# A hybrid decoder layer: a first phase ordered by a table of due times, attention's products weighted after the sum, w_out kept in the token tiles

## The chip, the cores and the metric

The kernel runs on one core of a Trainium2 chip. Five engines work from queues of their own: PE multiplies matrices (PEld is its loading of weights), DVE and ACT work on vectors, POOL on vectors and some DMAs, SP issues most DMAs. The metric is the device time of one execution in microseconds, the median of three runs.

## The reference

The layer works on 1024 tokens of width 1024, in fp32. It has an attention group and a gating group in parallel, an output projection with a residual, and then a mixture of experts, in which each token goes to 4 of 32 experts. What bears on this change is attention, which has three branches (compressed, selected, window) whose outputs are weighted by gates:

```python
h = rmsnorm(x, norm1_g)
z = h @ w_in                       # 1024 x 2328, split into q, k and v of three branches, gates, u, v
...
p_cmp = masked_softmax(s, dist_c >= 0)
o_cmp = jnp.einsum('bgrqc,bgcd->bgrqd', p_cmp.astype(vc.dtype), vc)
...
o_sel = jnp.einsum('bgrqk,bgqkd->bgrqd', p.astype(v_g.dtype), v_g)
...
o_win = jnp.einsum('bgrqk,bgkd->bgrqd', p.astype(v_w.dtype), v_w)
o = gt[..., 0:1] * o_cmp + gt[..., 1:2] * o_sel + gt[..., 2:3] * o_win
...
mixed = jnp.concatenate([rmsnorm(o_attn, out_norm_attn_g), rmsnorm(o_gm, out_norm_gm_g)], axis=-1)
x = x + mixed @ w_out
x = x + moe(rmsnorm(x, norm2_g), w_router, b_router, w_gate_up, b_gate_up, w_down, b_down)
```

There are 8 query heads of width 64 in two groups of 4, which share keys and values. With 16 selected blocks of 64 and 1024 tokens every block is selected, so the selected branch is causal attention over all keys; the window branch looks at the last 512.

## The kernel before, in words

Numbers are kept as a pair of f16 (a high part and the rest), so a product of fp32 accuracy takes three f16 matmuls; plain fp32 is used for transposes and small things.

*First phase.* The tokens are eight tiles of 128. `x_tile` normalises and transposes them into `xh` and `xl` (high and low parts). `piece_tile` projects them through w_in in nine pieces of columns, 24 matmuls of some 256 columns per tile and piece (lines 405 to 407). Keys and queries are normalised, transposed and stored (`stack_half`, `turn_half`).

*Attention* runs in units: one `Unit` is a group of 4 heads, a query tile i and a branch, 48 in all, in the order of `ORDER`. For each head `score` has two matmuls (lines 857, 858), and DVE adds distances and takes the running extreme (861); ACT takes the exponential with its sum (841). `weigh` divides the gate by the sum (878 to 880), and `scale` multiplies the four heads' probabilities by it, each on the engine that `SCALE` names (894 ACT, 896 DVE or POOL). `back` then does each block of 128 keys, 148 blocks in all: four fp32 transposes (910), an f16 high part on ACT (914) and low part on DVE (918), and the product with values (928, 929), with the values as the weights that PE loads and 512 columns (4 heads x 128 queries) streamed. The three branches of a group and tile add up in one PSUM bank; `finish` takes it out (942), transposes it back to tokens (946) and adds the two halves of the values' pair on DVE (950).

*Rows.* When both groups of a tile are done, `Rows` normalises, projects through w_out (`part`, lines 1255 to 1257), adds the residual, normalises again and routes. `out_row` (1045 to 1049) loads the eight blocks of w_out, scales and splits them into `wo`, a buffer that is opened in the place of the token tiles after the last projection (`open_out`). Gating runs beside it, on the columns u and v of the projection; its result goes to DRAM (`og_d`, line 559).

*Experts.* A second plan, of the same kind, does the experts (lines 1665 to 1817). Its weights come in as fp32 into five buffers, four of which lie in `wo`.

*What sets the order.* `Plan` records every operation with its engine, a cost, a due time, what it reads and writes, and the slots of rings that it uses: `psS` (3 PSUM banks for scores and projections), `psT` (3, for transposes), `psO` (2, for products), `par` (an arena of 15 blocks of probabilities) and others. `run` lays the operations out: among those that can start first on their engine, the one with the least due time. What it yields is each engine's queue, which the chip executes in order. Due times are written out in the code from a few constants (`TP`, `FS`, `AHEAD`, `US`, `WD`).

Of the kernel before, what the change touches and what calls it, by code (L numbers as in the profile page):

```python
# [61 lines left out]
ARENA = 15  # L62
# [8 lines left out]
SCALE = [['act', 'pool', 'pool', 'pool'], ['pool', 'dve', 'pool', 'act'], ['dve', 'dve', 'dve', 'act']]  # L71
MAXB = 64
LAND = 10.0

# [10 lines left out]
class Plan:  # L85
# [3 lines left out]
    def __init__(self, rings):  # L89
        self.rings = {k: (n, dyn, []) for k, (n, dyn) in rings.items()}  # L90
        self.ops, self.last, self.readers, self.scope = [], {}, {}, ()

# [19 lines left out]
    def op(self, eng, cost, fn, due, r=(), w=(), use=(), lag=None):  # L112
        i = len(self.ops)
        deps, take, after = set(), [], []
# [19 lines left out]
        self.ops.append((eng, cost, fn, due, deps, take, slots, after, lag))  # L134
# [7 lines left out]
    def run(self):  # L142
# [6 lines left out]
        end, free, avail = [0.0] * n, {}, {}  # L149
# [6 lines left out]
        def ready(i):  # L156
            eng, _, _, _, deps, take, _, after, _ = ops[i]
# [13 lines left out]
        for _ in range(n):  # L171
# [11 lines left out]
            eng, cost, fn, _, _, take, slots, _, _ = ops[i]  # L183
# [15 lines left out]
def layer_kernel(ctx: ExitStack, tc: tile.TileContext, x, norm1_g, w_in, q_norm_g, k_norm_g, cmp_pos,  # L199
# [22 lines left out]
    def rstd_of(dst, ss, n):  # L222
# [58 lines left out]
                     ph=(4, 1), pl=(4, 1), ob=(2, 1), mx=(8, 1), su=(6, 0), ptc=(4, 0), dup=(2, 0), par=(ARENA, 0),  # L281
                     m=(2, 0), ogt=(1, 0), x1=(2, 0), xn=(1, 0), xt=(1, 0), xp=(1, 0), s2=(2, 0), jo=(1, 1)))
# [10 lines left out]
    def rms(dst, src, n, tok, due, r):  # L293
        op("dve", 0.1, lambda: nc.vector.tensor_scalar(dst(), src(), 1.0 / n, EPS, op0=ALU.mult, op1=ALU.add), due, r=r, w=[tok])
        op("act", 0.1, lambda: nc.scalar.activation(dst(), dst(), AF.Sqrt), due, r=[tok], w=[tok])
# [3 lines left out]
    st = ExitStack()  # L299
    xtp = pool(st, "xtp")  # L300
    xh = xtp.tile([P, KD, T], F16, name="xh")
    xl = xtp.tile([P, KD, T], F16, name="xl")
# [28 lines left out]
    def x_tile(a):  # L331
        due = 1.5 * a
# [12 lines left out]
        op("act", 1.0, stat, due + 3, r=[x_], w=[ss])  # L345
        rms(lambda: rstd1[:, a:a + 1], lambda: ss1[:, a:a + 1], D, ("rstd1", a), due + 3.5, [ss])
        op("dve", 0.62, lambda: nc.vector.tensor_scalar(x_.t, x_.t, rstd1[:, a:a + 1], None, op0=ALU.mult), due + 4,
# [4 lines left out]
    def x_half(a, h, x_, due):  # L352
        b, tk = plan.slot("psT"), ("x", a, h)
        k, c = slice(4 * h, 4 * h + 4), slice(a * P, (a + 1) * P)
# [6 lines left out]
        op("act", 0.5, lambda: nc.scalar.activation(xh[:, k, c], four(b), AF.Copy, scale=SZ), due, r=[b], w=[tk])  # L361
        op("dve", 0.6, lambda: nc.vector.scalar_tensor_tensor(xl[:, k, c], four(b), SZ, xh[:, k, c], op0=ALU.mult,
                                                              op1=ALU.subtract), due, r=[b, tk], w=[tk])

    def piece_half(i, kh):
        _, c0, n, _ = PIECES[i]
# [17 lines left out]
        op("sp", 1.5, load, due - (14 if i else 0), w=[r])  # L384
        op("act", 1.6, hi, due - (8 if i else -3), r=[r, "g1"], w=[ws])
# [5 lines left out]
    def piece_tile(i, a, ws):  # L391
        kind, _, n, o0 = PIECES[i]
# [7 lines left out]
        def run():  # L400
            o = ps_tile(ps, psS)[:, :n]
            for k in range(KD):
                wh, wl = [v[:, k % 4, :n] for v in ws[k // 4].t]
                xa, xb = xh[:, k, a * P:(a + 1) * P], xl[:, k, a * P:(a + 1) * P]
# [7 lines left out]
    def take(kind, o0, a, ps, due):  # L412
        r, rs = 1.0 / (SW * SZ), ("rstd1", a)
        if kind == "v":
            op("act", 0.3, lambda: nc.scalar.activation(PO["vb"][:, a, o0:o0 + 256], ps.t[:, :256], AF.Identity, scale=r), due, r=[ps, rs],
# [3 lines left out]
        elif kind == "kcvc":  # L419
            op("act", 0.3, lambda: nc.scalar.activation(kcvc[:, a].rearrange("p b g d -> p (b g d)"), ps.t[:, :256], AF.Identity,  # L420
# [6 lines left out]
    def take_kv(br, a, ps, due, r, rs):  # L427
# [13 lines left out]
        op("act", 0.6, keys, due, r=[ps, rs], w=[("kv", br, a)])  # L441
# [3 lines left out]
        op("dve", 0.4, sums, due + 1, r=[("kv", br, a)], w=[("ssk", br, a)])  # L445
# [14 lines left out]
    def norms(lo, n, toks, key, due):  # L460
        rms(lambda: rsq[:, :, lo:lo + n], lambda: ssq[:, :, lo:lo + n], DH, ("rsq", key), due, toks)
# [69 lines left out]
    def gating(d0, due, late):  # L531
        def mask():
            nc.vector.tensor_scalar(PO["tril"], jp, 0.0, None, op0=ALU.is_ge)
# [1426 lines left out]
```

## Time and profile before

| | |
|---|---|
| median of 3 runs | 1983.84 us (1983.23 to 1987.50) |
| the profiled execution | 1987.46 us, of which the span is 1985.7 |
| granted clock of PE, mean of the span | 0.98 |
| busy in the span | PE 95%, PEld 85%, DVE 84%, ACT 75%, POOL 41% |
| first phase | to about 640 us; DMA moves 1 to 152 GB/s in its slices |
| experts | the rest; DMA about 300 to 360 GB/s |

Times within the profile are microseconds from the start of the span. "Busy" of PE includes the time in which the last columns of a burst run out, so it is more than the work done. The granted clock is a share of full speed, 2.4 GHz; 0.50 is the level of 1.2 GHz.

### The profile page before, as it was taken

Reading aid. Unit: us, or ns where it says so; the run is one execution under the profiler, and the core shown is the slowest. Engines: PE = TensorE matmul, PEld = TensorE weight load, DVE = VectorE, ACT = ScalarE, POOL = GpSimd, SP = SyncE. Lnnn points to the kernel's source line nnn. Section 1 sums busy time; section 2 is a strip of 40 time slices with the busy share of each in tenths; the row PEclk is TensorE's granted clock in tenths of the full one; section 3 lists DMA queues with packets and bytes.
Section 4 is the critical chain, followed back from the end, with each engine's and each line's share of the span. In section 5 each row is a group of like instructions: output and inputs, shape, how many; then the busy total and the mean of one; then the engine's idle time right before and its main releaser. Section 6 shows DMA issues by size and latency. Waiting matters only on the chain.

```text
span 1985.7 us, 58597 instructions
## 1 busy us (share of the span) xinstructions
PE 1879.5 (95%) x24346; PEld 1680.4 (85%) x24346; DVE 1659.9 (84%) x2876; ACT 1496.9 (75%) x2374; POOL 814.1 (41%) x699
## 2 busy tenths in 40 slices
PE   7999898989897899999999999999999999999996
PEld 6886666655554887899999999999999999999996
DVE  5668778787776899788989999899999999989883
ACT  6558868886653776677778888788888888878884
POOL 0212132354652255344444444344444525446442
PEclk9999999989998899999999999999999999999998
DMA  4320000033123998899999999999999999999993
GB/s 152 91 59 23 12 12 1 22 133 86 65 86 116 297 331 314 290 299 326 331 338 336 338 341 359 338 356 354 358 362 356 352 356 351 346 343 359 358 351 88
DMA packets 244768, 485.77 MB, mean 245 GB/s; under 512 B 20034, under 2 KB 29394, under 8 KB 244498
## 3 DMA queue, kind: packets, MB, share of 16 engines
q1 hardware_dynamic: 230658, 441.19, 63.1%
q0 software_dynamic: 12800, 40.79, 9.1%
q8 instruction: 192, 3.15, 0.6%
q14 instruction: 78, 0.64, 0.1%
q10 hardware_dynamic: 1040, 0.00, 0.0%
HBM read 450.94 MB, written 31.00 MB: 243 GB/s over the span
## 4 chain that ended last, share of the span: by engine, by line
PE 70%; DVE 10%; ACT 8%; DMA 7%; issue 3%; POOL 1%; DVEq 0%; POOLq 0%; SPq 0%; ACTq 0%
PE g L1739 16%; PE g L1740 16%; PE g L1741 16%; DMA wo<-in_w_gate_up_dram 3%; PE s L405 2%; PE s L407 2%; PE s L406 2%; DVE wl L1696 2%; ACT wh L1693 2%; DVE par L861 2%; PE b L910 2%; PE b L1807 2%; DMA wo<-in_w_down_dram 2%; PE b L1665 1%; DMA raw<-in_w_gate_up_dram 1%
## 5 line engine op out<-in xcount | busy, mean ns | idle before, releaser
L1739 PE MATMUL g<-xar,wh 128*128 128x88 f16 (+21 forms) x4096 | 772.3, 229 | 0.6 <-ACT ott L1790 0.6
L1740 PE MATMUL g<-xar,wh 128*128 128x88 f16 (+21 forms) x4096 | 772.5, 229 | 0.0
L1741 PE MATMUL g<-xar,wl 128*128 128x88 f16 (+21 forms) x4096 | 771.9, 229 | 0.0
L1696 DVE SCALAR_TENSOR_TENSOR wl<-wo,wh 128x2048 f16<-128x2048 f32 x308 | 715.2, 2328 | 39.2 <-ACT wh L1693 37.6
L1693 ACT ACTIVATE wh<-wo 128x2048 f16<-128x2048 f32 x308 | 625.9, 2036 | 160.3 <-PE g L1740 85.7
L1740 PEld LDWEIGHTS <-wh 128*128 128x128 f16 x6144 | 601.4, 98 | 15.4 <-issue 4.3
L1739 PEld LDWEIGHTS <-wh 128*128 128x128 f16 x6144 | 601.8, 98 | 10.7
L1741 PEld LDWEIGHTS <-wl 128*128 128x128 f16 x6144 | 601.3, 98 | 10.7
L1767 POOL TENSOR_TENSOR aar<-t,aar 128x136 f16<-128x136 f32 (+21 forms) x256 | 360.3, 1426 | 477.6 <-ACT aar L1765 447.9
L1739 PE MATMUL g<-aar,wh 128*128 128x120 f16 (+21 forms) x2048 | 385.1, 228 | 3.1 <-DVE t L1754 3.1
L1741 PE MATMUL g<-aar,wl 128*128 128x120 f16 (+21 forms) x2048 | 385.1, 228 | 0.0
L1740 PE MATMUL g<-aar,wh 128*128 128x120 f16 (+21 forms) x2048 | 385.1, 228 | 0.0
L1754 DVE TENSOR_SCALAR t<-g,bias 128x120 f32<-128x120 f32 (+20 forms) x512 | 170.6, 363 | 33.4 <-PE g L1741 21.4
L1693 ACT ACTIVATE wh<-raw 128x2048 f16<-128x2048 f32 x76 | 154.7, 2035 | 40.2 <-PE g L1740 23.5
L1696 DVE SCALAR_TENSOR_TENSOR wl<-raw,wh 128x2048 f16<-128x2048 f32 x76 | 176.5, 2322 | 7.8 <-ACT wh L1693 7.4
L1817 POOL DMA_INDIRECT out_dram<-orow,ix x51 | 121.6, 2384 | 146.9 <-ACT orow L1810 82.0
L1635 POOL DMA_INDIRECT xg<-xn_d,ix x51 | 127.0, 2491 | 112.2 <-PE g L1741 35.9
L405 PE MATMUL s<-wh,xh 128*128 128x256 f16 (+1 forms) x576 | 158.8, 276 | 2.8 <-DVE mx L861 1.9
L407 PE MATMUL s<-wh,xl 128*128 128x256 f16 (+1 forms) x576 | 158.6, 275 | 0.1
L406 PE MATMUL s<-wl,xh 128*128 128x256 f16 (+1 forms) x576 | 158.7, 275 | 0.0
L896 POOL TENSOR_SCALAR par<-par,su 128x384 f32<-128x384 f32 (+7 forms) x32 | 60.0, 1884 | 151.9 <-DVE su L880 68.2
L918 DVE TENSOR_TENSOR pl<-b,ph 128x512 f16<-128x512 f32 (+1 forms) x148 | 96.8, 682 | 30.0 <-ACT ph L914 29.5
(388 smaller groups left out, 2888.4 us busy)
## 6 DMA issues: line engine op xcount, KB each, us to landing
wo<-in_w_gate_up_dram SPq DMA_DIRECT2D x205, 1024.0 KB
wo<-in_w_down_dram SPq DMA_DIRECT2D x103, 1024.0 KB
raw<-in_w_gate_up_dram SPq DMA_DIRECT2D x51, 1024.0 KB
raw<-in_w_down_dram SPq DMA_DIRECT2D x25, 1024.0 KB
wr<-in_w_in_dram SPq DMA_DIRECT2D x16, 512.0 KB
xs<-in_x_dram SPq DMA_DIRECT2D x8, 512.0 KB
x<-in_w_out_dram SPq DMA_DIRECT2D x8, 512.0 KB
x<-in_x_dram SPq DMA_DIRECT2D x8, 512.0 KB
```

The lines of the kernel that those rows point to most:

```text
L405: mm(o, xa, wh, start=(k == 0), stop=False)
L406: mm(o, xa, wl, start=False, stop=False)
L407: mm(o, xb, wh, start=False, stop=(k == KD - 1))
L1635: nc.gpsimd.indirect_dma_start(out=xg.t[:w], out_offset=None, in_=xn_d, in_offset=bass.IndirectOffsetOnAxis(ap=ix.t[:w, 0:1], axis=0))
L1693: nc.scalar.activation(ws.v[0], raw_.v, AF.Copy, scale=SW)
L1696: nc.vector.scalar_tensor_tensor(ws.v[1], raw_.v, SW, ws.v[0], op0=ALU.mult, op1=ALU.subtract)
L1739: mm(o, wh, xa, start=(kh == 0 and k == 0), stop=False)
L1740: mm(o, wh, xb, start=False, stop=False)
L1741: mm(o, wl, xa, start=False, stop=(kh == 1 and k == 3))
L1754: nc.vector.tensor_scalar(t.t[:, s, :c], ps[s].t[:, :c], self.bias(2 * h + s), m, op0=ALU.add, op1=o)
L1767: plan.op("pool", 0.9 + c / 440, lambda: nc.gpsimd.tensor_tensor(out=self.a[:, h, 1], in0=t.t[:, 1, :c], in1=self.a[:, h, 0], op=ALU.subtr ...
L1817: self.plan.op("pool", 2.0, lambda: nc.gpsimd.indirect_dma_start(out=out, out_offset=bass.IndirectOffsetOnAxis(ap=ix.t[:w, 0:1], axis=0), ...
```

## The change

Three things change, all in the first phase; the plan of the experts is left alone, except that four of its five fp32 buffers now lie in the token tiles.

1. *Order.* Operations are put in groups (`plan.group()`), and each group has an offset in a table `WHEN`, which is added to its due times (the offsets lie between about -2300 and 1530 us). The costs in the plan are set to other numbers, and a switch of ACT's function table costs 1.29 us in the plan.
2. *Weights.* `scale` is gone. The probabilities are transposed and split unscaled. In the product the probabilities are now what PE loads, and the values (128 columns, both parts of the pair) are streamed: 8 matmuls of 128 columns a block. Each unit has a product bank of its own, in the layout of tokens; `weighted` multiplies it by the ratio on DVE, and `finish` adds three of them and the two halves on POOL. The ring of results has 4 slots, and the arena of probabilities 13 blocks instead of 15.
3. *w_out.* Tokens are kept tile by tile in `xw`, which stays open. `out_row` writes the split w_out over a token tile once the last projection has read it, and loads through the ring of the projection weights.

```diff
-ARENA = 15
+ARENA = 13
-SCALE = [['act', 'pool', 'pool', 'pool'], ['pool', 'dve', 'pool', 'act'], ['dve', 'dve', 'dve', 'act']]
+OB = 4
+WHEN = [
+    1346.1, 299.4, 788.3, -170.5, 1081.8, 114.3, -565.0, 519.3, -380.7, 1232.6, -82.9, 90.6, -610.6, 327.8, 529.5, -374.5, 361.1,
...
+TABLE = 1.29
...
+    def group(self):
+        self.at += 1
...
     def op(...):
         i = len(self.ops)
+        due += self.when[self.at] if self.at < len(self.when) else 0
...
+            if table not in (None, loaded):
+                loaded, cost = table, cost + TABLE
...
-            plan.op("dve", 0.25, ratio, due, r=[("su", su, j) for j in range(4)] + ["gates"], w=[su])
-            for j in range(4):
-                self.scale(j, due)
-
-        def scale(self, j, due):
-            su, nk = self.su, self.nk
-            eng = SCALE[self.br][j]
-            def run():
-                p, w = self.probs(j), su.t[:, j:j + 1]
-                if eng == "act":
-                    nc.scalar.activation(p, p, AF.Copy, scale=w)
-                else:
-                    (nc.gpsimd if eng == "pool" else nc.vector).tensor_scalar(p, p, w, None, op0=ALU.mult)
...
+            plan.op("dve", 0.41 if br else 0.61, ratio, due, r=[("su", su, j) for j in range(4)] + ["gates"], w=[("w", su)], use=[su])
...
             def hi():
-                nc.scalar.activation(ph.t[:n], four(b)[:n], AF.Copy)
+                nc.scalar.activation(ph.t[:n], four(b)[:n], AF.Copy, scale=SP)
             def lo():
-                nc.vector.tensor_tensor(out=pl.t[:n], in0=four(b)[:n], in1=ph.t[:n], op=ALU.subtract)
+                nc.vector.scalar_tensor_tensor(pl.t[:n], four(b)[:n], SP, ph.t[:n], op0=ALU.mult, op1=ALU.subtract)
             def pv():
...
-                mm(o.t, va, ph.t[:n].rearrange("p h t -> p (h t)"), start=st, stop=False)
-                mm(o.t, va, pl.t[:n].rearrange("p h t -> p (h t)"), start=False, stop=en)
+                for j in range(4):
+                    for m, p in enumerate((ph, pl)):
+                        mm(o.t[:, j * P:(j + 1) * P], p.t[:n, j], va, start=st and j + m == 0, stop=en and j + m == 4)
...
-    def finish(g, i, o, due):
+        def weighted(self, due):
+            ob, o, su = self.ob, self.o, self.su
+            def run():
+                ob.t = PO["hp"].tile([P, 4, P], F32, name="ob", bufs=OB)
+                nc.vector.tensor_tensor(out=ob.t, in0=four(o), in1=su.t[:, :, None].to_broadcast([P, 4, P]), op=ALU.mult)
+            plan.op("dve", 0.6, run, due, r=self.parts + [("w", su)], w=[ob], use=[o, su])
+
+    def finish(g, i, units, due):
-        def evac():
-            nc.scalar.activation(ob.t, o.t, AF.Copy, scale=1.0 / (SP * SV))
-        def turn():
-            for j in range(4):
-                nc.tensor.transpose(four(b)[:, j], ob.t[:, j * P:(j + 1) * P], ident)
-        plan.op("dve", 0.65, lambda: nc.vector.tensor_reduce(
...
+        a, b, c = [u.ob for u in units]
+        def last():
+            v = a.t.rearrange("p h (s d) -> p h s d", s=2)
+            nc.gpsimd.tensor_tensor(out=zq[:, i, 256 * g:256 * g + 256].rearrange("p (h d) -> p h d", h=4), in0=v[:, :, 0], in1=v[:, :, 1],
+                                    op=ALU.add)
+        for x in (b, c):
+            plan.op("pool", 1.56, lambda x=x: nc.gpsimd.tensor_tensor(out=a.t, in0=a.t, in1=x.t, op=ALU.add), due, r=[x], w=[a])
+        plan.op("pool", 0.9, last, due, r=[a] + ..., w=[("o", g, i)])
...
+    def wo(k, s):
+        return xw[:, (k + 4) % 8, s].rearrange("p k t -> p (k t)")
     def out_row(k, due):
-        r, g = plan.slot("x1"), gms[:, k:k + 1]
+        r, g, a = plan.slot("wr"), gms[:, k:k + 1], (k + 4) % 8
...
+           w=[("wo", k), ("x", a, 0), ("x", a, 1)])
...
-        PO["wo"] = pool(ctx, "raw").tile([P, 4, 2, 2, D], F16, name="wo")
...
-    raws = [PO["wo"][:, n].rearrange("p s j f -> p (s j f)").bitcast(F32) for n in (2, 3, 0, 1)] + [raw5]
+    raws = [xw[:, 2 * n:2 * n + 2].rearrange("p a s k t -> p (a s k t)").bitcast(F32) for n in range(4)] + [raw5]
```

PE's queue at the first product of the first unit, before (`ph` and `pl` are the parts of the transposed probabilities, `vv` the values, `kcs` and `q` keys and queries, `o` the product's bank):

```order
L910 MATMUL b_2465<-ident_81,par_1604 128x128 x4
L928 LDWEIGHTS vv_103
L928 MATMUL o_2471<-ph_2415,vv_103 128x512
L929 LDWEIGHTS vv_103
L929 MATMUL o_2471<-pl_2456,vv_103 128x512
L857 LDWEIGHTS q3_154
```

The same place now (`xw` is a token tile, `wh` and `wl` projection weights):

```order
L470 LDWEIGHTS xw_119
L470 MATMUL s_2246<-wh_1713,xw_119 128x256
L996 LDWEIGHTS ph_2236
L996 MATMUL o_2278<-vv_103,ph_2236 128x128
L996 LDWEIGHTS pl_2271
L996 MATMUL o_2278<-vv_103,pl_2271 128x128
```

Two products of 512 columns with two loads became eight of 128 with a load each (the last four rows come four times, once for each head).

POOL's queue where attention begins, before (`par` and `ptc` hold probabilities, `su` the ratios; the rows ahead are a normalisation):

```order
L476 TENSOR_TENSOR rsq_106<-nwq_107 128x8x4
L896 TENSOR_SCALAR par_1604<-par_1604,su_1959 128x384 x2
L896 TENSOR_SCALAR ptc_1961<-ptc_1961,su_2004 128x64 x3
L896 TENSOR_SCALAR par_1604<-par_1604,su_2008 128x128 x2
L896 TENSOR_SCALAR ptc_2002<-ptc_2002,su_2014 128x64 x3
L896 TENSOR_SCALAR par_1604<-par_1604,su_2422 128x768 x2
```

The same place now (`ob` are weighted products, `zq` the attention output):

```order
L541 TENSOR_TENSOR rsq_106<-nwq_107 128x8x4
L1025 TENSOR_TENSOR ob_2409<-ob_2409,ob_2528 128x512
L1025 TENSOR_TENSOR ob_2409<-ob_2409,ob_2560 128x512
L1021 TENSOR_TENSOR zq_99<-ob_2409 128x256
L1025 TENSOR_TENSOR ob_2639<-ob_2639,ob_2699 128x512
```

POOL no longer stands between the exponentials and the transposes; it comes after the products.

SP's queue around w_out, before (`wr` projection weights, `og_d` the gated result in DRAM, `ogt` its way back):

```order
L372 DMA wr_3520<-in_w_in_dram 128x4x256
L559 DMA og_d_66<-vb_1618 128x4x512 x2
L1045 DMA x1_5561<-in_w_out_dram 128x1024
L1045 DMA x1_5581<-in_w_out_dram 128x1024
L1143 DMA ogt_5651<-og_d_66 128x512
L1143 DMA ogt_5708<-og_d_66 128x512
L1045 DMA x1_5716<-in_w_out_dram 128x1024
```

The same place now:

```order
L433 DMA wr_3542<-in_w_in_dram 128x4x256
L1123 DMA wr_3586<-in_w_out_dram 128x1024
L1123 DMA wr_3781<-in_w_out_dram 128x1024
L1123 DMA wr_4697<-in_w_out_dram 128x1024
L1123 DMA wr_4815<-in_w_out_dram 128x1024
L1123 DMA wr_4867<-in_w_out_dram 128x1024
L628 DMA og_d_66<-vb_1707 128x4x512
L1123 DMA wr_5026<-in_w_out_dram 128x1024
L1123 DMA wr_5093<-in_w_out_dram 128x1024
L1123 DMA wr_5219<-in_w_out_dram 128x1024
L628 DMA og_d_66<-vb_1707 128x4x512
```

Five loads of w_out stand ahead of the first store of the gated result and three between the two, where before both stores came first.

## Rows read from the trace of the kernel before

**Rows 1.** Instructions of three lines: count, duration in ns (min/median/max), first and last start.

```profile
L928 PE MATMUL o<-ph,vv x132: 376/379/634, 175.0 to 594.7; 128*128 128x512 f16 x132
...
L405 PE MATMUL s<-wh,xh x576: 269/273/421, 14.4 to 401.7; 128*128 128x256 f16 x171, 128*128 128x280 f16 x21
...
L1739 PE MATMUL g<-xar,wh x4096: 192/223/364, 654.6 to 1952.8; 128*128 128x136 f16 x19, 128*128 128x120 f16 x15, 128*128 128x160 f16 x14, 128*128 128x88 f16 x13
```

**Rows 2.** Windows: busy us (instructions) of PE, PEld, DVE, ACT, POOL; clock, DMA, GB/s.

```profile
175.00:596.00 421.00, 383.24 (x2652) 254.55 (x2649) 318.54 (x961) 317.74 (x749) 175.78 (x289) 0.97 0.15 49
596.00:655.00 59.00, 39.98 (x302) 26.77 (x301) 40.03 (x105) 24.10 (x38) 12.25 (x9) 0.76 0.45 156
...
700.00:1985.70 1285.70, 1256.11 (x19410) 1220.71 (x19407) 1151.66 (x1393) 1013.97 (x1267) 582.63 (x344) 0.99 0.98 332
```

**Rows 3.** Timeline near 570 us: start, duration in us, engine, line, operation.

```profile
569.78 0.38 PE L1257 MATMUL s<-wo,ml 128*128 128x512 f16 x1
569.99 0.38 PE L1255 MATMUL s<-wo,mh 128*128 128x512 f16 x1
...
571.29 0.61 PE L1339 MATMUL b<-iden,xp 128*128 128x128 f16 x8
...
571.68 0.10 PEld L928 LDWEIGHTS <-vv 128*128 128x128 f16 x1
571.74 0.38 PE L928 MATMUL o<-ph,vv 128*128 128x512 f16 x1
```

**Rows 4.** The chain that ended last, near 290 us: start, us, what.

```profile
290.43 0.44 PE b L946 x4
```

**Rows 5.** PE's groups by shape, 175 to 596 us: count, busy us, mean ns, idle before.

```profile
L910 PE MATMUL b<-ident,par 128*128 128x128 f32 x514 | 75.3, 279 | 13.2 <-DVE pl L918 8.9 <-DVE zq L950 1.6 <-DVE mx L861 1.0
L405 PE MATMUL s<-wh,xh 128*128 128x256 f16 x224 | 61.0, 273 | 1.9 <-DVE mx L861 1.9
...
L929 PE MATMUL o<-pl,vv 128*128 128x512 f16 x132 | 52.0, 394 | 3.3 <-DVE pl L918 3.2
...
L1255 PE MATMUL s<-wo,mh 128*128 128x512 f16 x96 | 36.9, 384 | 0.3 <-DVE mx L861 0.2
```

**Rows 6.** Waits, 0 to 600 us: who for whom, us in total, times, longest.

```profile
ACT ph L914 <- PE b L910: 32.2, 34, 3.7
...
PE b L910 <- DVE pl L918: 10.1, 10, 2.4
```

**Rows 7.** The line that loads w_out: durations in ns, first and last start.

```profile
L1045 SPq DMA_DIRECT2D x<-in_w_out_dram x8: 327/332/1010, 408.0 to 443.6; - x8
```

**Rows 8.** Windows, 420 to 430 us.

```profile
420.00:430.00 10.00, 5.99 (x21) 3.44 (x20) 8.02 (x22) 6.26 (x13) 7.96 (x19) 0.50 0.39 135
```

**Rows 9.** Groups of the first phase, 0 to 650 us: count, busy us, mean ns, idle before.

```profile
L896 POOL TENSOR_SCALAR par<-par,su 128x384 f32<-128x384 f32 (+7 forms) x32 | 60.0, 1884 | 151.9 <-DVE su L880 68.2 <-PE o L928 30.8 <-ACT ph L914 27.6
...
L896 DVE TENSOR_SCALAR par<-par,su 128x640 f32<-128x640 f32 (+7 forms) x64 | 32.7, 549 | 0.9
...
L894 ACT ACTIVATE par<-par,su 128x640 f32<-128x640 f32 (+7 forms) x32 | 23.1, 732 | 6.4 <-DVE su L880 6.4
...
L950 DVE TENSOR_REDUCE zq<-b 128x256 f32<-128x512 f32 x16 | 11.0, 687 | 9.5 <-PE b L946 9.5
...
L753 DVE TENSOR_TENSOR dup<-zq,rsq 128x512 f32<-128x512 f32 x16 | 10.5, 691 | 10.1 <-POOL rsq L476 5.7 <-PE b L766 4.3
...
L946 PE MATMUL b<-ident,ob 128*128 128x128 f32 x64 | 10.0, 281 | 0.4 <-ACT ob L942 0.4
...
L942 ACT ACTIVATE ob<-o 128x512 f32<-128x512 f32 x16 | 9.4, 588 | 2.3 <-PE o L929 2.0
L611 POOL TENSOR_TENSOR vb<-vb,ubuf 128x1024 f32<-128x1024 f32 x4 | 9.4, 2352 | 21.5 <-ACT ubuf L610 21.5
```

**Rows 10.** PE's groups by shape, 550 to 600 us.

```profile
L1255 PE MATMUL s<-wo,mh 128*128 128x512 f16 x34 | 12.9, 379 | 0.2 <-DVE mx L861 0.2
```

**Rows 11.** Windows, 550 to 600 us.

```profile
550.00:600.00 50.00, 47.84 (x326) 28.68 (x324) 36.83 (x108) 31.60 (x63) 31.08 (x46) 1.00 0.27 95
```

More of the change, by code (lines that the diff above doesn't have):

```diff
@@ L133, in op @@
         lag = lag if lag is not None else 2.25 if eng == "sp" else 0.25
-        self.ops.append((eng, cost, fn, due, deps, take, slots, after, lag))
+        self.ops.append((eng, cost, fn, due, deps, take, slots, after, lag, table))
     def swap(self, fn, due, closes, opens):
@@ L331, in x_tile @@
     def x_tile(a):
+        plan.group()
         due = 1.5 * a
@@ L352, in x_half @@
     def x_half(a, h, x_, due):
+        plan.group()
         b, tk = plan.slot("psT"), ("x", a, h)
-        k, c = slice(4 * h, 4 * h + 4), slice(a * P, (a + 1) * P)
+        xh, xl = [xw[:, a, s, 4 * h:4 * h + 4] for s in range(2)]
         def turn():
@@ L391, in piece_tile @@
     def piece_tile(i, a, ws):
+        plan.group()
         kind, _, n, o0 = PIECES[i]
@@ L489, in run @@
                 nc.vector.tensor_scalar(u() if i == 2 else y(), z(), 1.5, y(), op0=ALU.add, op1=ALU.mult)
-        op("dve", 1.4, run, due, r=list(r), w=[tok])
+        op("dve", 1.87, run, due, r=list(r), w=[tok])
     def q_norms(o0, due):
+        plan.group()
         lo = o0 // DH
@@ L531, in gating @@
     def gating(d0, due, late):
+        plan.group()
         def mask():
@@ L545, in gelu @@
                 nc.scalar.activation(v, v, AF.Gelu_apprx_tanh)
-        op("act", 6.0, gelu, due, r=["gmc"], w=toks)
+        plan.group()
+        op("act", 3.8, gelu, due, r=["gmc"], w=toks, table="gelu")
         row_sums(due, toks)
@@ L563, in spatial @@
     def spatial(g, due, wsr):
+        plan.group()
         b = plan.slot("psT")
@@ L572, in row_sums @@
     def row_sums(due, toks):
+        plan.group()
         junk = plan.slot("ubuf")
@@ L585, in normed @@
     def normed(a, due, toks):
+        plan.group()
         v = lambda: PO["vb"][:, a]
@@ L637, in compress @@
     def compress(s_, due):
+        plan.group()
         w1 = plan.slot("w1")
@@ L714, in compress_end @@
     def compress_end(due):
+        plan.group()
         def sums():
@@ L821, in front @@
         def front(self, j):
+            plan.group()
             g, i, br, nk = self.g, self.i, self.br, self.nk
@@ L1132, in mix @@
         def mix(self):
+            plan.group()
             a, due, end = self.a, self.due - 12, self.end
@@ L1180, in proj @@
         def proj(self):
+            plan.group()
             zs = [plan.slot("psS") for _ in range(2)]
@@ L1261, in add @@
         def add(self, z, nh):
+            plan.group()
             x1, c = self.x1, slice(nh * 512, nh * 512 + 512)
@@ L1397, in layer_kernel @@
             gating_end(start(i + 1))
+    plan.scope = ("Z",)
+    for n in range(8):
+        out_row((n + 4) % 8, start(9) + WO + 4 * n)
     plan.swap(open_out, 0, ["Z"], ["W0"])
```

201 lines of the change are left out of this document (105 added, 96 removed), and 47 rows, old and new, of the table WHEN.

## The prediction, made before the changed kernel was run

> **What bounds the kernel now.** I read the first and last starts of three lines first, since they cut the program into parts: the first and the last product of attention weights with values start at 175.0 and 594.7 us, the last projection of the tokens at 401.7, and the first product of the experts at 654.6 [rows 1]. The table by windows then shows three kinds of stretch [rows 2]. From 700 us on PE is busy 98% of the time and nothing there is touched. From 596 to 655 a serial tail runs with the granted clock at 0.76. Between, from 175 to 596, PE is busy 383 of 421 us, DVE 319, ACT 318 and POOL 176. A busy PE is not a PE at its peak, since the end of each burst is counted too, so I count that stretch's work by columns. Back to back, a 512-column f16 matmul follows the one before after 0.2155 us (0.421 ns a column) [rows 3], and four fp32 transposes take 0.44 us, 0.11 each [rows 4]. By the counts by shape [rows 5] the stretch holds 514 transposes at L910 (56 us), 3 x 224 projection matmuls of 256 columns (72), 2 x 132 products of 512 columns (57) and 3 x 96 output-projection matmuls (62); the smaller shapes, priced in the same way, add 103. That is 350 us of work in 421: a density of 0.83. Some 70 us of PE are lost there, to waits. The first phase is thus not bound by one engine: PE, DVE and ACT hand blocks around through three small PSUM rings, and each waits for the others (ACT's evacuation L914 waits 32.2 us for PE in all, PE's transposes 10.1 us for DVE, in 10 waits [rows 6]).
>
> The worst place has its own rows: the eight loads of w_out are issued between 408.0 and 443.6 us, after the last projection, and at 420 to 430 PE is busy 6.0 of 10 us at a granted clock of 0.50, the 1.2 GHz level [rows 7, 8].
>
> **The change, part by part.** *Weighting the products.* The scaling of the probabilities goes: on ACT 23.1 us, on DVE 32.7, on POOL 60.0, with the short rows of the compressed branch on top. So does the old finish: 9.4 us of ACT (L942), 11.0 of DVE (L950) and 64 fp32 transposes of PE (L946), at 0.11 each 7.0 us [rows 9]. Added are 48 multiplications on DVE, PSUM times a broadcast scalar column. No row shows that form; a 128x512 tensor-tensor on DVE takes 0.69 us (L753 [rows 9]), so 33 us, with 0 and twice that as far ends. POOL gets 32 additions of 128x512 and 16 folds to 128x256: a 128x1024 tensor-tensor takes it 2.35 us (L611 [rows 9]), so an addition 1.2 and a fold 0.6 if time goes by size, up to 1.8 and 0.9 by half again: 48 to 72 us. Net: ACT -32 us, DVE -11, PE -7, and POOL about as before. As important is a chain: a block's transposes used to wait for sums, reciprocal and scaling by three engines, with POOL taking 1.9 us on average for one head [rows 9]; now they need only the exponential, and the reciprocal has until the unit's last product. Beside the chain, these freed times lie on engines that are not full; by themselves they are worth only what the waits give back.
>
> *Product turned round.* Each of the 148 blocks had 2 matmuls of 512 columns (0.431 us) and now has 8 of 128 columns with 8 weight loads. The same shape is in the trace: 8 f16 matmuls of 128 columns at L1339, each with its own load, start at 571.29 and the next line's matmul starts at 571.74: 0.45 us for eight, 56 ns each [rows 3]. So +0.019 x 148 = +2.8 us. Far ends: 0, and loads that hide behind nothing. One load shows 0.10 us [rows 3]; eight make 0.80, which is +0.37 x 148 = +55 us. I take +2.8, since the row has exactly this shape. The Trainium skill speaks against this: the page "TensorE: Matmul & The Clock Gate", section "Back-to-back issue gap", gives about 81 ns per pair of load and matmul of 128 columns in a sustained stream. By that figure eight take 0.65 us, the product would cost +32 us of PE, and my sum would come to 1972; the eight transposes above ran at 56 ns, so by this trace the rule does not bind in so short a burst.
>
> *Order by a table.* Each group of operations gets its own offset to its due time, and the costs that the planner lays out are set anew. Nothing is added on any engine; what changes is which ready instruction stands first in each queue. The trace cannot show the new density; it shows what densities this mix reaches. At 550 to 600 us the mix of output projection and attention holds 34 matmuls at each of L1255 to L1257 (22.0 us) [rows 10], and the other shapes in it, priced alike, 24.3: 46.3 of 50, or 0.93. DVE is there at 37 of 50 and ACT at 32 [rows 11], against 76% for both over the whole stretch [rows 2]: PE is dense where ACT is light. With ACT 32 us lighter and no scaling in the chain, I take 0.92. PE's work there becomes 350 - 6.6 (60 of the transposes lie in it) + 2.8 = 346 us; at 0.92 it lasts 376 us instead of 421: **-45**. At the old 0.83 it lasts 417 (-4); at 0.96, which no such stretch shows, 360 (-61). DVE would then be busy 308 of 376, or 82%: next in line, but not the bound.
>
> *w_out in the token tiles' place.* The loads pass, in SP's queue, ahead of the two stores of the gated tile, and use the projection weights' ring. They and their 16 splits can run before the last projection is over. What hid nothing at 408 to 430 is covered by other work; this is inside the density above and not counted again. The price is a store and a load in one queue: in the new order three loads stand behind the first store, which waits for POOL's gate product, and output projection waits for them. If that product is late, so is the first token row. The arena for probabilities shrinks from 15 to 13 blocks; a token block with 8 + 5 blocks then fills it alone. I take 0 for both, since the planner's order was laid with them, and -0 to +6 as ends (the longest waits of PE that the table of waits lists for one place).
>
> *Tail.* Old: evacuation 0.59, four transposes 0.44, reduction 0.69 [rows 4, 9]: 1.7 us. New: DVE 0.69, a POOL addition 1.2 to 1.8, a fold 0.6 to 0.9: 2.5 to 3.4. So **+1** (0.8 to 1.7), on the path, once. The experts' stretch, 1331 us from 654.6, starts when the order of experts is known, and is unchanged: 0, with 3 us either way for how the first loads fall.
>
> Sum: 1985.7 - 45 + 1 = 1941.7 of span; the profiled execution lasted 1987.46, 1.8 us beyond its span, so 1943.5. The median of the three runs shown is 1983.84, 3.6 below that, and the forecast against it is **1940**.
>
> **The rivals.** *Loads pace the turned product (0.07).* If eight loads cannot run ahead, the product is slower by up to 55 us of PE, as above; at half exposure, 28, the stretch lasts (346 + 28) / 0.92 = 407, and the run about 1971. For it: PEld is busy 255 us of the stretch already [rows 2]. Against it: the burst at 571.29.
> *The order is no denser (0.08).* In-order queues meet durations that differ from the plan, and density stays at 0.83: -4 + 1, or 1981. For it: the old order was planned too and reached 0.83. Against: the scaling chain and the hole at 408 to 430 are gone.
> *Half of it (0.15).* Density 0.87 to 0.88: 346 / 0.875 = 395, or -26 + 1: 1959.
> *Denser (0.10).* 0.96: about 1924. For it: every group has its own due time, and fillers (projections, then output projections) are there almost throughout. Against it: DVE would be busy 308 of 360.
> *The product banks turn into the wait (0.07), slower.* Two PSUM banks hold products. They were handed on 16 times, by ACT; now 48 times, by DVE, after the reciprocal and behind what stands in DVE's queue. PE's queue is in order, so a product that waits for a bank holds back scores, transposes and projections behind it. PE's waits for DVE at the transposes are 1.0 us on average and 2.4 at the longest [rows 6]. At 1.2 us exposed, between these, for each of 48 units this costs 58 us against 44 gained: 1998. It decides from 44 / 48 = 0.9 us each. Against it: two banks alternate, and a unit has up to eight blocks in which the other bank can come free.
>
> **How the numbers follow.** The forecast's own case (density 0.89 to 0.94, so 1930 to 1955) has 0.53. This kernel's measurement tells about 0.2%, 4 us, from no change. Faster by more: 0.53 + 0.15 + 0.10 + 0.07, and a little of the case at 1981, makes 0.87. Within it: 0.06. Slower: 0.07. A range of 1920 to 1968 leaves out part of the denser case, the cases at 1971 and 1981 and the slower one, some 0.2 in all.
>
> **What would show it.** From the first to the last product 375 to 380 us instead of 421, with 8 products of 128 columns in about 0.45 us; no long waits of PE for the banks; the loads of w_out begun before the last projection; the granted clock of that stretch near 1.0 instead of 0.97; 1331 us from the first expert product to the end. I am wrong in the mechanism if PE's gaps come back in front of the products, and in the size if density lies outside 0.89 to 0.94.

## The result, and the profile after

The changed kernel takes 1961.85 us (median of 4 runs, 1959.60 to 1963.94), against 1985.67 for the kernel before (4 runs). The ratio is 0.9878, with a 95% interval of 0.9856 to 0.9900. The forecast was 1940, and the time lies where the rival "Half of it" stood (1959). The profiled execution of the changed kernel lasted 1960.88 us with a span of 1959.1, 26.6 less than the span before.

First the lines that cut the program, as in [rows 1]: the first part of the product, the last projection of tokens, the output projection, the experts. Columns: count, duration in ns (min/median/max), first and last start.

```profile
L996 PE MATMUL o<-vv,ph x528: 217/219/315, 159.9 to 571.0; 128*128 128x128 f16 x176
...
L996 PE MATMUL o<-vcs,ph x64: 215/216/228, 176.2 to 575.9; 64*128 64x128 f16 x64
...
L468 PE MATMUL s<-wh,xw x576: 269/273/418, 16.4 to 352.2; 128*128 128x256 f16 x171, 128*128 128x280 f16 x21
...
L1337 PE MATMUL s<-xw,mh x128: 376/379/391, 394.1 to 594.9; 128*128 128x512 f16 x128
...
L1826 PE MATMUL g<-xar,wh x4096: 192/223/342, 629.8 to 1926.2; 128*128 128x136 f16 x19, 128*128 128x120 f16 x15, 128*128 128x160 f16 x14, 128*128 128x88 f16 x13
```

Set against the starts of before, the 26.6 us come from four places: the first product starts 15.1 earlier (159.9, was 175.0); from there to the last product it takes 416.0 us (was 420.6 to the last small one at 595.6, so -4.6); from the last product to the first of the experts 53.9 (was 59.0, -5.1); the experts 1329.3 (was 1331.1, -1.8). The forecast had 375 to 380 in the second place and nothing in the first. The two are not independent: counted by columns as in the prediction, the time before the first product holds 143.5 us of work instead of 151.0, at a density of 0.90 instead of 0.86. So some 9 of the 15 us are work that moved behind the first product, and 6 are density.

Now the windows that answer to [rows 2]; columns as there. The third and fourth are the place where projections have run out and output projections have not begun (the hole, below); the fifth is its last part, the sixth and seventh are what lies ahead of it and behind it.

```profile
160.00:576.00 416.00, 385.31 (x3568) 293.12 (x3565) 330.69 (x991) 301.42 (x724) 150.54 (x267) 0.98 0.17 54
576.00:630.00 54.00, 35.99 (x279) 24.82 (x277) 36.72 (x103) 22.36 (x35) 9.36 (x9) 0.74 0.41 146
352.00:379.00 27.00, 21.23 (x228) 16.64 (x225) 23.09 (x75) 24.97 (x63) 9.91 (x36) 1.00 0.26 89
379.00:394.00 15.00, 13.49 (x82) 12.06 (x82) 9.09 (x36) 8.02 (x22) 4.96 (x6) 0.66 0.54 104
384.00:394.00 10.00, 9.36 (x45) 8.28 (x46) 5.12 (x19) 6.20 (x18) 1.26 (x1) 0.52 0.66 118
160.00:352.00 192.00, 181.56 (x1770) 149.84 (x1768) 156.25 (x439) 154.47 (x360) 33.69 (x46) 1.00 0.12 37
394.00:576.00 182.00, 169.02 (x1495) 114.57 (x1493) 142.26 (x448) 113.96 (x281) 101.99 (x179) 0.99 0.18 62
```

PE is busy 385 of 416 us, but counted by shape and priced as in the prediction (0.421 ns a column, 0.11 us an fp32 transpose) the stretch holds 355 us of work: 0.854, where 0.92 was forecast. (A transpose of 32 columns counts 0.11 as well, since the 32 at L1148 take 3.5 us; an fp32 matmul of 512 columns counts 0.44, since two of them at L670 take 0.86.) The stretch before holds 351 of 421 by the same count, the prediction's 0.83. The 42 us from 352 to 394 hold 27.7 (0.66) and the remaining 374 us hold 327.5 (0.88). The hole of [rows 8] has thus not gone. It has moved ahead by some 45 us: before, the 34 us from 400 to 434 held 18.2 (0.54).

The hole loses 14 us of PE, and not all of it is waiting: in its last 10 us PE is busy for 9.36 us at a mean granted clock of 0.52, close to the 1.2 GHz level. That half clock is about 5 of the 14.

What the end of the hole is made of shows in the chain that ended last (start, us, what), from 376 us on:

```profile
376.57 5.17 DMA ogt<-og_d
...
381.82 0.73 ACT ogt L1231
...
382.60 0.67 PE b L1248 x4
...
383.29 0.60 ACT mh L1253
383.89 0.71 ACT x L1163 x2
...
384.64 3.61 PE b L1153 x16
388.25 1.04 PE b L1248 x4
```

The first row of tokens comes back from DRAM (`ogt`), is scaled, transposed and split; between its two halves PE has sixteen small transposes of the experts' biases (L1153) that take 3.61 us, and no attention work stands between them. And this is what SP issued (timeline; start, us):

```profile
350.66 0.33 SPq L1123 DMA_DIRECT2D wr<-in_w_out_dram  x1
360.29 0.38 SPq L628 DMA_DIRECT2D og_d<-vb  x1
375.11 0.81 SPq L1139 DMA_DIRECT2D x<-in_b_gate_up_dram  x2
...
376.57 7.11 SPq L1223 DMA_DIRECT2D ogt<-og_d  x2
```

The last load of w_out goes out at 350.66, before the last projection, as forecast. But its last split, on DVE, starts only at 373.3, behind eight steps of L939 (distances) for other units, and the buffers of the rows open after it: SP stands from 360.7 to 375.1. That looked like the cause; the first experiment tests it.

Groups and waits that answer to [rows 5], [rows 9] and [rows 6]: count, busy us, mean ns of one, idle before; then who waits for whom, us in total, times, longest. The first two lines are of 160 to 576 us.

```profile
L976 PE MATMUL b<-ident,par 128*128 128x128 f32 x520 | 75.6, 279 | 12.7 <-DVE pl L984 9.0 <-DVE mx L939 2.9 <-ACT par L919 0.4
...
L996 PE MATMUL o<-vv,pl 128*128 128x128 f16 x528 | 70.3, 221 | 8.3 <-DVE pl L984 8.3
...
L1025 POOL TENSOR_TENSOR ob<-ob 128x512 f32<-128x512 f32 x32 | 40.7, 1270 | 191.9 <-DVE ob L1009 164.9 <-DVE su L959 20.4 <-DVE mx L939 6.3
L1009 DVE TENSOR_TENSOR ob<-o,su 128x512 f32<-128x512 f32 x48 | 32.5, 686 | 7.4 <-PE o L996 6.6 <-POOL nw L538 0.3
L1021 POOL TENSOR_TENSOR zq<-ob 128x256 f32<-128x256 f32 x16 | 12.0, 748 | 1.2
```

```profile
ACT ph L980 <- PE b L976: 33.7, 31, 4.2
...
PE b L976 <- DVE pl L984: 9.0, 11, 1.7
PE o L996 <- DVE pl L984: 8.6, 7, 3.4
```

The new operations cost what was estimated (686 ns on DVE, 1270 and 748 on POOL). No product waits for a bank, only for `pl`, 7 times. POOL's long waits are those of an engine with nothing else to do.

### The profile page after: what moved, and what is told of

It is laid out like the page before. It is cut to its first block, busy times and chain, and to the rows that moved or that the text cites. A ratio compares the mean times of both kernels' runs of the same rounds, so it can differ in the third digit from the quotient of the medians.

```text
span 1959.1 us, 60049 instructions
## 1 busy us (share of the span) xinstructions
PE 1865.3 (95%) x25170; PEld 1708.0 (87%) x25170; DVE 1653.5 (84%) x2844; ACT 1468.2 (75%) x2310; POOL 783.0 (40%) x667
## 4 chain that ended last, share of the span: by engine, by line
PE 75%; DVE 9%; DMA 7%; ACT 5%; issue 3%; POOL 1%; SPq 0%; DVEq 0%; POOLq 0%; ACTq 0%
PE g L1826 16%; PE g L1827 16%; PE g L1828 16%; PE s L468 3%; PE s L469 3%; PE s L470 3%; DVE par L939 3%; DMA xw<-in_w_gate_up_dram 2%; PE b L1894 2%; PE b L976 2%; PE o L996 2%; DVE wl L1783 2%; DMA raw<-in_w_gate_up_dram 2%; ACT wh L1780 2%; PE b L1752 1%
## 5 line engine op out<-in xcount | busy, mean ns | idle before, releaser
L1783 DVE SCALAR_TENSOR_TENSOR wl<-xw,wh 128x2048 f16<-128x2048 f32 x308 | 714.4, 2326 | 40.2 <-ACT wh L1780 34.6
L1780 ACT ACTIVATE wh<-xw 128x2048 f16<-128x2048 f32 x308 | 626.4, 2036 | 157.2 <-PE g L1827 86.9
L1841 DVE TENSOR_SCALAR t<-g,bias 128x120 f32<-128x120 f32 (+20 forms) x512 | 170.8, 364 | 32.5 <-PE g L1828 22.4
L468 PE MATMUL s<-wh,xw 128*128 128x256 f16 (+1 forms) x576 | 158.2, 275 | 1.2 <-DVE mx L939 1.1
L469 PE MATMUL s<-wl,xw 128*128 128x256 f16 (+1 forms) x576 | 158.1, 275 | 0.0
L470 PE MATMUL s<-wh,xw 128*128 128x256 f16 (+1 forms) x576 | 158.0, 274 | 0.0
L1025 POOL TENSOR_TENSOR ob<-ob 128x512 f32<-128x512 f32 x32 | 40.7, 1270 | 191.9 <-DVE ob L1009 164.9
L1849 DVE SCALAR_TENSOR_TENSOR t<-t 128x136 f32<-128x136 f32 (+21 forms) x256 | 100.4, 402 | 18.1 <-ACT t L1846 15.1
```

The source lines that it names most:

```text
L468: mm(o, xa, wh, start=(k == 0), stop=False)
L469: mm(o, xa, wl, start=False, stop=False)
L470: mm(o, xb, wh, start=False, stop=(k == KD - 1))
L1780: nc.scalar.activation(ws.v[0], raw_.v, AF.Copy, scale=SW)
L1783: nc.vector.scalar_tensor_tensor(ws.v[1], raw_.v, SW, ws.v[0], op0=ALU.mult, op1=ALU.subtract)
L1841: nc.vector.tensor_scalar(t.t[:, s, :c], ps[s].t[:, :c], self.bias(2 * h + s), m, op0=ALU.add, op1=o)
```

## The experiments

In most of them each engine's queue must stay as it was but for the edit. For that the order that the planner laid is written into the kernel as a list of its operations (2418 in the changed kernel, 2562 in the one before), and the planner takes it from there:

```diff
+LAID = [ ... ]
...
-        for _ in range(n):
+        for turn in range(n):
+            i = LAID[turn]
```

The experts' part, which no edit touches, lasts 1324 to 1340 us in the profiles of these runs (1329.3 in the changed kernel). An edit in the first phase is therefore read in two ways: by the time, and by the start of the first product of the experts in the profiled execution, which is 654.6 us before and 629.8 in the changed kernel.

**1. The last split of w_out where its block lands.** In `LAID` the two operations of the last `out_row` move, so that in the trace ACT's part starts at 356.8 us (was 365.1) and DVE's at 359.0 (was 373.3).

> Every queue as in the changed kernel, but the last split of w_out (one ACT and one DVE instruction) stands where its block has just landed, some 8 and 16 us earlier. Theory 'new wait': the rows' buffers open at about 359 us instead of 374, the bias loads go out at 361 instead of 375, the first output projection starts 10 to 14 us earlier than 394, and the kernel gains 8 to 12 us against the changed one (about 1951). Rival 'the hole moves': PE's queue meets the same gap a little later, since what stands behind the output projection waits for other things; 0 to 3 us, about 1960.

Measured: 1969.79 (1959.01 to 1973.93), ratio 0.9930 (0.9909 to 0.9951): no gain, and in the median 8 us more than the changed kernel takes. The trace is of the execution of 1959.01; the other four took 1965.94 to 1973.93, and what made them longer it does not show. SP's timeline shows that the wait is gone, and PE's that this brings nothing:

```profile
362.22 1.49 SPq L1139 DMA_DIRECT2D x<-in_b_gate_up_dram  x2
...
365.79 20.89 SPq L1223 DMA_DIRECT2D ogt<-og_d  x2
```

```profile
381.11 4.10 PE L1148 MATMUL b<-ident,x 32*128 32x32 f32 x32
385.14 1.11 PE L1248 MATMUL b<-ident,ogt 128*128 128x128 f32 x4
387.64 3.62 PE L1153 MATMUL b<-ident,x 32*128 32x32 f32 x16 [1.39 <-ACT x L1163]
391.19 1.11 PE L1248 MATMUL b<-ident,zq 128*128 128x128 f32 x4
```

The bias loads go out 13 us earlier and the first `ogt` load 11, yet PE comes to the first of these transposes at 381.1 (379.0 in the changed kernel), since attention stands ahead of it in its queue. The first output projection starts at 396.2 (394.1), the first product of the experts at 633.3 (629.8). The theory of the new wait falls: taking this wait away gains nothing.

**2. An empty table.**

```diff
-WHEN = [ ... ]
+WHEN = []
```

> The changed kernel with an empty table: products, w_out and costs as changed, order by the written due times. Theory 'the table carries the gain': 1980 to 2000, the last product at 590 to 610 us. Rival 'the weighting and w_out carry half of it': about 1970, the last product near 583.

Measured: 2015.64 (2014.88 to 2016.44), ratio 1.0152 (1.0133 to 1.0171). Both expectations said less. Weighting and w_out without the table are 30 us slower than before; with it 24 faster. The main row of its products:

```profile
L948 PE MATMUL o<-vv,ph x528: 216/219/314, 166.9 to 619.0; 128*128 128x128 f16 x176
```

**3. Two wide matmuls in place of eight.**

```diff
-                for j in range(4):
-                    for m, p in enumerate((ph, pl)):
-                        mm(o.t[:, j * P:(j + 1) * P], p.t[:n, j], va, start=st and j + m == 0, stop=en and j + m == 4)
+                mm(o.t, va, ph.t[:n].rearrange("p h t -> p (h t)"), start=st, stop=False)
+                mm(o.t, va, pl.t[:n].rearrange("p h t -> p (h t)"), start=False, stop=en)
...
-                nc.vector.tensor_tensor(out=ob.t, in0=four(o), in1=su.t[:, :, None]..., op=ALU.mult)
+                nc.vector.tensor_tensor(out=ob.t, in0=four(o), in1=gates[:, self.i]...[:, :, None]..., op=ALU.mult)
```

> Every queue as in the changed kernel, but a block's product is again two matmuls of 512 columns with the values as what PE loads (the banks then hold heads by tokens, and the multiplication after them takes the gates, so the attention values are not the layer's). Theory 'term of +2.8 us right': 1184 small matmuls become 296 wide ones and the stretch from first to last product shortens by 0 to 4 us. Rival 'loads pace the product': by 20 us or more.

Measured: 1963.54 (1958.75 to 1971.39), ratio 0.9894 (0.9860 to 0.9928), the same as the changed kernel. First and last product:

```profile
L994 PE MATMUL o<-ph,vv x132: 376/379/551, 159.4 to 569.5; 128*128 128x512 f16 x132
L994 PE MATMUL o<-ph,vcs x16: 386/386/387, 175.6 to 574.3; 64*128 64x512 f16 x16
```

159.4 to 574.3, 414.9 us, against 416.0: the turned product costs about 1 us by these two traces. The rival of the loads, 28 to 55 us, falls.

**4. Without DVE's low part.**

```diff
-                pl.t = PO["hp"].tile([P, 4, P], F16, name="pl")
-                nc.vector.scalar_tensor_tensor(pl.t[:n], four(b)[:n], SP, ph.t[:n], op0=ALU.mult, op1=ALU.subtract)
+                pl.t = ph.t
```

> Every queue as in the changed kernel, but DVE's low part of the probabilities is left out (148 instructions, some 100 us of DVE); the product reads the high part twice, so PE's work is the same. Theory 'handing over through DVE holds PE': the stretch from first to last product falls from 416 us to 395 or less. Rival 'PE's own order and the hole at 350 to 395 hold it': it falls by less than 8 us.

Measured: 1956.34 (1951.62 to 1957.93), ratio 0.9848 (0.9825 to 0.9871).

```profile
352.00:379.00 27.00, 21.55 (x220) 18.33 (x220) 15.57 (x67) 21.98 (x60) 13.05 (x41) 0.95 0.27 85
```

```profile
L996 PE MATMUL o<-vv,ph x1056: 217/219/230, 160.1 to 561.0; 128*128 128x128 f16 x176
L996 PE MATMUL o<-vcs,ph x128: 216/216/227, 176.3 to 565.9; 64*128 64x128 f16 x128
```

From first to last product 405.8 us, 10 less, between what the two theories said. The first product of the experts starts at 620.2, 9.6 earlier; the experts' part is 6 us longer in this execution, so the time as a whole shows some 5. In the hole PE does not become denser (19.0 us of work from 352 to 379, 18.9 in the changed kernel) though DVE falls from 23.1 to 15.6 of 27 us. Some 100 us of DVE are worth 10 here: DVE is a part of what holds PE, not the bound.

**5 to 8. Other orders.** An order was searched at random: due times of single operations are shifted, the planner lays the order, and the shift is kept if the planner's last operation ends earlier. Two of its numbers were set anew. One engine hands on to the next after 0.46 us instead of 0.25, the value with which the planner's own times for the first and last product and the first output projection come near those of the trace. A group of bias transposes costs 1.8 us instead of 0.95, since the 32 at L1148 take 3.5 us at the full clock. Runs 5 and 6 hold the instructions of the kernel before and of the changed kernel, each in such an order; 7 and 8 move the biases and give them buffers of their own (not shown in the diff). Run 7 is in the changed kernel's order with the early split of run 1, run 8 in a searched one.

```diff
-    biases(start(9) + BD)
...
     for a in range(NT):
         x_tile(a)
+    biases(0)
```

> The kernel before, instruction for instruction, but its first phase stands in an order searched anew: with the costs of the changed kernel, 0.46 us instead of 0.25 from one engine to the next, and 1.8 us for each group of the bias transposes. Weighting, product and w_out are the old ones. Theory 'the order alone carries the gain': 1935 to 1955, the last product near 555 us. Rival 'without the weighting moved, the chain through POOL keeps PE waiting': 1970 or more.

> The changed kernel, instruction for instruction, in an order searched in the same way (0.46 us from engine to engine, 1.8 us for each group of bias transposes). Theory 'the order in the table was laid for hand-overs that are too short': 1930 to 1948, the first output projection near 383 us instead of 394, the last product near 550 instead of 576. Rival 'the work itself allows no denser order': 1955 to 1965.

> Every queue as in the changed kernel, but the biases' load, their 48 small transposes and their store stand at 25 to 45 us, in buffers of their own, and the last split of w_out stands as in the first experiment. Theory 'the small transposes make the hole at 379 to 394': they cost some 6 us early, the hole's 15 us go; 4 to 10 us faster than the changed kernel. Rival 'the hole is the start of the rows, and PE waits there whatever stands in it': 0 to 6 us slower.

> The changed kernel with the biases at the start in buffers of their own, in an order searched with 0.46 us from engine to engine. Theory of the order: 1932 to 1952, beside the run before it; the place of the biases makes less than 5 us between the two. Rival 'the biases are the hole': 10 us faster than that run.

Measured: run 5 1957.95 (1955.95 to 1961.59), ratio 0.9855 (0.9829 to 0.9882); run 6 1951.77 (1951.20 to 1956.61), 0.9835 (0.9806 to 0.9863); run 7 1970.08 (1960.59 to 1975.17), 0.9904 (0.9867 to 0.9941); run 8 1966.87 (1965.34 to 1969.85), 0.9909 (0.9882 to 0.9936).

Run 5 (its lines are 7 higher than those of before): the old instructions, with POOL's scaling in the chain, the old finish and w_out loaded after the projections, in a time not above that of the changed kernel. It is 3 us above the range of its theory and 12 below its rival.

```profile
L935 PE MATMUL o<-ph,vv x132: 377/379/634, 173.0 to 569.2; 128*128 128x512 f16 x132
...
L412 PE MATMUL s<-wh,xh x576: 269/273/421, 16.1 to 370.1; 128*128 128x256 f16 x171, 128*128 128x280 f16 x21
...
L1262 PE MATMUL s<-wo,mh x128: 376/379/390, 411.5 to 590.6; 128*128 128x512 f16 x128
```

Run 6 lies between its theory and its rival. The hole is there, shallower, from the last projection to the first output projection:

```profile
L468 PE MATMUL s<-wh,xw x576: 269/273/417, 17.4 to 360.9; 128*128 128x256 f16 x170, 128*128 128x280 f16 x22
...
L1337 PE MATMUL s<-xw,mh x128: 376/379/390, 399.6 to 585.3; 128*128 128x512 f16 x128
```

By columns these 38.7 us hold 29.7 us of work (0.77), where the changed kernel's 41.9 hold 27.6 (0.66). Both ends are later than in the changed kernel and against what was expected; the gain is not in an earlier start of the rows. From its first product at 170.3 to its last at 567.2 the density is 0.88.

Run 7: with the biases out of the hole the hole stays, so these transposes are not its cause either. Between the starts below lie 38.8 us with 22.5 of work; the biases' 5.3 are gone from it, and what is left is as in the changed kernel.

```profile
L470 PE MATMUL s<-wh,xw x576: 269/273/283, 16.6 to 358.2; 128*128 128x256 f16 x171, 128*128 128x280 f16 x21
...
L1339 PE MATMUL s<-xw,mh x128: 376/379/631, 397.0 to 597.6; 128*128 128x512 f16 x128
```

The median is 8 us above the changed kernel, but 0.3 above run 1, whose early split it has as well, and the first product of the experts starts at 633.5 (633.3 in run 1): moving the biases by itself gained and lost nothing that shows.

Run 8 is above the range of its theory and 15 us behind run 6, where less than 5 was expected: either the place of the biases costs, or this order came out worse. One order does not tell.

**9 to 12. Is that the order or the instructions?** Two more searched orders for each set of instructions, with other starts of the search and the same time for each (the edit is another `LAID`).

> The changed kernel, instruction for instruction, in a second searched order (0.46 us from engine to engine; another start of the random search). Theory 'what an order leaves is decided by the order, not by products or w_out': 1945 to 1965, overlapping with the orders of the kernel before. Rival 'weighting and w_out are worth something beside a good order': faster than both orders of the kernel before, by 5 us or more.

> As the run before it, a third searched order of the changed kernel. Theory: 1945 to 1965. Rival: 5 us or more below the orders of the kernel before.

> The kernel before, instruction for instruction, in a second searched order (same costs, same search). Theory 'the order alone decides': 1945 to 1970, overlapping with the orders of the changed kernel. Rival: slower than all of these by 5 us or more.

> The kernel before in a third searched order. Theory: 1945 to 1970, overlapping with the orders of the changed kernel. Rival: slower than all of these by 5 us or more.

| searched orders | medians, us | ratios to before | first product of the experts, us |
|---|---|---|---|
| instructions of the changed kernel (6, 9, 10) | 1951.77, 1951.76, 1957.81 | 0.9835, 0.9826, 0.9862 | 619.2, 615.7, 617.0 |
| instructions of before (5, 11, 12) | 1957.95, 1977.65, 1962.92 | 0.9855, 0.9949, 0.9872 | 626.1, 643.1, 627.1 |

Run 11 is slower than its theory allowed (1945 to 1970). By the medians runs 9, 11 and 12 meet the 5 us of their rivals, run 10 does not. All three of the first row lie below all three of the second, by 0.1 at the closest (1957.81 and 1957.95) and by 12 in the mean (1953.8 against 1966.2). By the ratios, which compare each with the kernel before beside it, the rows overlap (0.9862 for run 10, 0.9855 for run 5) and differ by 10 us in the mean. The first phase alone, in one trace of each, keeps them apart: by 6.9 us at the closest and by 15 in the mean. Orders of the same instructions differ by up to 20 us, so with three of each the size of this difference is uncertain: that weighting and w_out help a good order is likely; by how much, and which of the two does it, is not shown. The order alone gives the old instructions 9 to 28 us.

Run 9 beats both kernels: 1951.76 (1950.91 to 1952.57), ratio 0.9826 (0.9810 to 0.9842), 10 us below the changed kernel.

## Why the forecast was right in direction and not in size

*The step that failed* is "I take 0.92". The density of PE's work from the first to the last product is 0.854, outside the 0.89 to 0.94 that the prediction set for itself. The 0.92 was read from the 50 us from 550 to 600 alone. Windows of the kernel before, columns as in [rows 2], of which the last is the 50 us ahead of those:

```profile
175.00:400.00 225.00, 206.37 (x1504) 147.28 (x1502) 170.92 (x513) 181.17 (x444) 61.64 (x72) 0.99 0.03 10
400.00:434.00 34.00, 24.33 (x138) 15.26 (x137) 27.61 (x91) 28.78 (x68) 17.81 (x53) 0.80 0.37 125
434.00:596.00 162.00, 152.54 (x1013) 92.02 (x1011) 120.01 (x359) 107.79 (x241) 96.32 (x165) 0.98 0.27 87
500.00:550.00 50.00, 44.63 (x304) 26.82 (x303) 34.56 (x110) 30.48 (x71) 31.05 (x64) 0.97 0.16 58
```

By columns, as everywhere above, the same mix of output projection and attention holds 41.0 us of work from 500 to 550 (0.82) and 0.88 over all of 434 to 596; the window chosen was its best. Beside it stand 0.84 while projections last and 0.54 in the hole. In the changed kernel these are 0.90 (160 to 352), 0.66 (the hole) and 0.86 (394 to 576). The gain in density lies where projections fill, and behind the hole PE is no denser than before, although output projections are there to fill.

That makes the 40 us between 376 and 416, a little rounded. The stretch holds 355 us of work and not 346, most of it moved in from ahead of the first product: 10 us at 0.92. The hole, at the rest's 0.88, would last 32 us instead of 42: 10. And the rest is 0.88 instead of 0.92: 20. What holds the rest at 0.88 stays open; DVE's low part is some of it (4).

By the prediction's sign for a wrong mechanism (gaps of PE in front of the products) it stands between: PE stands 8.7 us there, all for `pl`, and stood 3.3 before [rows 5]; in front of the transposes of full blocks it stands 12.7 and stood 13.2. So taking the scaling out of the chain has not visibly shortened PE's waits at the transposes.

*"The hole at 408 to 430 is covered by other work"* failed with it, and this is the part that the profile could have shown. The hole stands between two kinds of filler (work that waits for nothing). From the last projection to the first output projection it is 42 us in the changed kernel (352.2 to 394.1), 32 before (401.7 to 433.6), 41 in run 5 and 39 in runs 6 and 7. There attention is nearly alone, and in the first 27 us of it ACT is busy 25.0 and DVE 23.1 in the changed kernel while PE waits for blocks; in the last 10 PE works at about half clock. Loading w_out earlier gives PE nothing to do there. What exactly ends it stays open: not the last split (1), not the biases (7), not DVE's low part (4); an order can make it shallower (6).

*What was not in the sum at all*: the 15.1 us ahead of the first product. The table moves work behind it and makes what stays there denser; both were counted as if they stood still. That the time came out near a case of the prediction is therefore luck: the stretch gave 4.6 us, and 22 came from places that the sum put at 0 or at +1.

*Weighting.* Its costs were right to a few us: 32.5 of DVE for the 48 multiplications (33 estimated), 40.7 and 12.0 of POOL (48 to 72 for both). That the shorter chain by itself makes PE denser is not shown: without the table it is 30 us slower than before (2), though that order was laid for nothing in particular, and with a searched order the difference to the old chain is 10 to 15 us in the mean of three, together with that of w_out.

*Product.* +2.8 was forecast, and 1 is what run 3 allows. The burst of eight is as it was read from L1339 [rows 3]; here it is at 371.7 us, in the timeline (start, us):

```profile
371.71 0.22 PE L996 MATMUL o<-vv,ph 128*128 128x128 f16 x1
371.76 0.22 PE L996 MATMUL o<-vv,pl 128*128 128x128 f16 x1
371.82 0.22 PE L996 MATMUL o<-vv,ph 128*128 128x128 f16 x1
371.87 0.22 PE L996 MATMUL o<-vv,pl 128*128 128x128 f16 x1
```

That is 55 ns for a pair of load and matmul. The Trainium skill's 81 ns ("TensorE: Matmul & The Clock Gate", section "Back-to-back issue gap") is for a sustained stream; these bursts of 8 to 32 run faster, and the measurement decides.

*w_out* at 0, with +6 as the far end: run 1 takes its only visible wait away and gains nothing, so nothing speaks against 0, but no run has w_out's move alone. No row shows the +6: the longest of the waits in [rows 6] that are PE's is 2.4. *Tail*: +1 forecast, -5.1 measured from last product to first expert product; which part of the 5 is the order and which the new finish was not tried. *Experts*: within 2 us, as forecast.

*The rivals.* "The product banks turn into the wait" did not happen: PE never waits for `ob`. "The order is no denser" nearly holds for the stretch from first to last product taken alone (0.854 after 0.833), and not for the kernel, since the same order gained 15 us ahead of it. "Half of it" had the right time with a density of 0.87 to 0.88; it is 0.88 outside the hole only.

## What to carry to other kernels

The density of the best 50 us of a trace is not the rate of a phase, not even of the same mix: here the 50 us ahead of them had 0.82. Count several windows of each mix before one is carried over, mark where each kind of filler begins and ends, and price the gaps between them apart. Where a change brings a new order together with new instructions, give the old instructions an order of the same kind: here that alone brought 9 to 28 us, where the whole change brought 24.

## What the runs showed of the hardware

From 379 to 394 us PE counts as busy for 13.5 of 15 us, and yet its granted clock is 0.66 on average. The small transposes of that time show both levels (groups of the first phase: count, busy us, mean ns, idle before):

```profile
L1153 PE MATMUL b<-ident,x 32*128 32x32 f32 x16 | 3.6, 398 | 1.4 <-ACT x L1163 1.4
L1148 PE MATMUL b<-ident,x 32*128 32x32 f32 x32 | 3.5, 279 | 0.0
```

The 32 take 0.110 us each, as much as a transpose of 128 columns; the 16 that come some 2 us later take 0.226. The granted clock is 1.00 up to 383 us, 0.66 in the microsecond from 383 and 0.50, the 1.2 GHz level, from 384 to 393, in a stretch that "busy" calls nearly full. PE had stood for 1.4 us up to 384.6; whether that or the thinner work of the 30 us ahead of it brought the clock down, no run separates. And a queue that is only handed its work earlier does not run it earlier: with the loads 11 to 13 us ahead (1), PE came to the transposes that need them 2 us later.
